# A first node as sixteen direct products, and a two-step node order at the start of a causal convolution on TensorE

**Chip, cores, metric.** One core of one Trainium2 chip. The metric is the device time of one execution in microseconds (us), median of several runs; "span" is the time from the first to the last instruction in the profiled execution, 1.7 to 3 us shorter. The mean granted TensorE clock of all runs used here lay between 0.993 and 1.000 of full speed.

## The reference

```python
# x: (8, 4096, 512) float32, kernel: (8, 512, 512) float32
out = np.zeros_like(x)
for k in range(8):
    shifted = x if k == 0 else np.concatenate(
        [np.zeros((B, k, D)), x[:, :-k, :]], axis=1)
    out += np.matmul(shifted, kernel[k])
```

A causal convolution over the sequence with eight taps, each tap a 512 x 512 matrix.

## The kernel before

Each of 128 partitions owns a run of 256 rows, worked off in 32 steps of eight rows. Within a step the 8 x 8 tap products are split three times in the Karatsuba manner: LO (taps 4 to 7), HI (taps 0 to 3) and MID, whose weights are differences of a HI and a LO weight. A step has three nodes of nine products, 27 instead of 64. A product is four matmuls of 128x512.

```python
def product(bank, comp, w, start):
    for c in range(DC):
        nc.tensor.matmul(bank, lhsT=comp[:, c * P:(c + 1) * P], rhs=w[:, c, :], ...)

def node_a1(k):                       # first product of node k
    ...
    n.q = pair(3)
    product(n.q[:, 1], n.s[1][1], W[a, MID, HI], True)
    nc.scalar.copy(out=n.q[:, 0], in_=n.q[:, 1])
```

Then come two products (`a0`, `u`), ScalarE copies that seed two PSUM pairs and fill `dts`, a buffer that the subtractions read, two more products (`v`) with a VectorE subtraction each (`d`), and four last ones (`l`). VectorE builds the sums of x rows (D4, D42, D1, D2 ...) and most of the middle weights. Halo rows are the seven rows before a partition's run; fills are matmuls with zeros at the start. x is loaded by GpSimd into `xin`, cast to bf16, and transposed by a DMA into one tile, used for every step again:

```python
XT = spool.tile([P, K, D], bf, name="XT")            # 8 rows, two halves
def transpose_x(xin, h):
    nc.sync.dma_start_transpose(out=XT[:, 4 * h:4 * h + 4, :]..., in_=xin...)
def prep_m():                                        # sums for the MID node
    tt(D1[:, 0:2], XT[:, 7::-7], XT[:, 0:2], ADD)
    ...
order = [(0, LO), (0, HI), (0, MID)]
order += [(i, a) for i in range(1, NIT) for a in (MID, LO, HI)]
```

Of the kernel before, what the change touches and what calls it, by code (L numbers as in the profile page):

```python
# [22 lines left out]
def kernel(  # L23
# [47 lines left out]
    F2 = spool.tile([P, 2, D], bf, name="F2")  # L71
    F21 = spool.tile([P, 4, D], bf, name="F21")
    F1 = spool.tile([P, 2, D], bf, name="F1")
    F0 = spool.tile([P, D], bf, name="F0")

# [3 lines left out]

    def load_x(i, h):  # L80
        xin = xpool.tile([P, 4, D], bf, name="xin")
        nc.gpsimd.dma_start(out=xin, in_=xr[:, K * i + 4 * h:K * i + 4 * h + 4, :])  # L82
        return xin

    def transpose_x(xin, h):
        nc.sync.dma_start_transpose(
            out=XT[:, 4 * h:4 * h + 4, :].rearrange("p j (c m) -> p (j c) m", m=P),
            in_=xin.rearrange("p j d -> p (j d)"))
# [47 lines left out]
    nc.gpsimd.dma_start(out=H[1:P, 4:8], in_=xr[0:P - 1, RUN - 4:RUN, :])  # L136
    x0 = [load_x(0, 0)]
    nc.gpsimd.dma_start(out=H[1:P, 1:4], in_=xr[0:P - 1, RUN - 7:RUN - 4, :])  # L138
# [12 lines left out]
    def load_w(tap):  # L151
        n = K - 1 - tap
        nc.gpsimd.dma_start(out=W[n >> 2, n >> 1 & 1, n & 1], in_=kr[:, :, tap, :])

    def mid_a(b_, c_):
        return W[MID, b_, c_], W[HI, b_, c_], W[LO, b_, c_]

    def mid_b(a, c_):
        return W[a, MID, c_], W[a, HI, c_], W[a, LO, c_]

    def mid_c(a, b_):
        return W[a, b_, MID], W[a, b_, LO], W[a, b_, HI]

    def by_dve(o, u, v):
        tt(o, u, v, SUB)

    def by_pe(o, u, v, prs):
        for h in range(2):
            pw = pair(prs[h])
            for k in range(2):  # L170
                nc.tensor.matmul(pw[:, k], lhsT=ident, rhs=u[:, 2 * h + k], start=True, stop=False)
                nc.tensor.matmul(pw[:, k], lhsT=identn, rhs=v[:, 2 * h + k], start=False, stop=True)
            nc.scalar.copy(out=o[:, 2 * h:2 * h + 2], in_=pw)

    for tap in (6, 4, 7, 5):
        load_w(tap)
    x0.append(load_x(0, 1))
    for tap in (2, 0, 3, 1):
        load_w(tap)
# [6 lines left out]
    def transpose_pe(src, k):  # L186
        o = pair(k).bitcast(bf).rearrange("p a (b d) -> p (a b) d", b=2)
        for t in range(4):
            for c in range(DC):
                nc.tensor.transpose(o[:, t, c * P:(c + 1) * P], src[:, t, c * P:(c + 1) * P], ident)  # L190
        return o

    def x_at(t):
        return (x0[0][:, t], ident) if t >= 0 else (H[:, 8 + t], identh)

    def sums_pe(k, *sums):

        pw = pair(k)
        for h, ts_ in enumerate(sums):
            for c in range(DC):  # L200
                for n, t in enumerate(ts_):
                    src, idt = x_at(t)
                    nc.tensor.matmul(pw[:, h, c * P:(c + 1) * P], lhsT=src[:, c * P:(c + 1) * P],  # L203
                                     rhs=idt, start=n == 0, stop=n == len(ts_) - 1,
                                     skip_group_check=True)
        return pw
# [4 lines left out]
    o = transpose_pe(x0[0], 0)  # L211
    nc.scalar.copy(out=XT[:, 0:4], in_=o)
    pw = sums_pe(1, (-4, 0), (-3, 1))
    nc.vector.tensor_copy(out=D4[:, 0:2], in_=pw)  # L214
    pw = sums_pe(2, (-2, 2), (-1, 3))
    nc.vector.tensor_copy(out=D4[:, 2:4], in_=pw)
    pw = sums_pe(3, (-5, -1))
    nc.vector.tensor_copy(out=D4[:, 7], in_=pw[:, 0])
    pw = sums_pe(0, (-7, -3), (-6, -2))
    nc.scalar.copy(out=D4[:, 5:7], in_=pw)  # L220
    prep_d41(LO)
    pw = sums_pe(1, (-1, 0), (0, 1))
    nc.scalar.copy(out=F1, in_=pw)
    fill(pair(3))
    tt(D42[:, 7], D4[:, 5], D4[:, 7], ADD)
    prep_d42(LO)
    pw = sums_pe(2, (-2, 0), (0, 2))
    nc.scalar.copy(out=F2, in_=pw)
    pw = sums_pe(0, (-3, -2, -1, 0), (-2, -1, 0, 1))
    nc.scalar.copy(out=F21[:, 0:2], in_=pw)  # L230
    by_dve(*mid_b(LO, HI))
    pw = sums_pe(1, (-1, 0, 1, 2), (0, 1, 2, 3))
    nc.scalar.copy(out=F21[:, 2:4], in_=pw)
    nc.scalar.copy(out=F0, in_=XT[:, 0])
    fill(pair(0))
    fill(pair(1))
    prep_d421(LO)
    by_dve(*mid_c(LO, LO))
    by_dve(*mid_b(LO, LO))
    by_dve(*mid_c(LO, MID))  # L240
    by_dve(*mid_c(LO, HI))
    xi = [load_x(1, 0)]

    mpool = ctx.enter_context(tc.tile_pool(name="m", bufs=2))
    cpool = ctx.enter_context(tc.tile_pool(name="c", bufs=2))
    ypool = ctx.enter_context(tc.tile_pool(name="y", bufs=4))
# [7 lines left out]

    class Node:
        pass

    def streams(i, a):

        if a == MID and i == 0:  # L260
            return (F0, [F1[:, 0], F1[:, 1]], [F2[:, 0], F2[:, 1]],
# [4 lines left out]
        o = 4 * a  # L266
        return (D4[:, o], [D41[:, 2 * a], D41[:, 2 * a + 1]], [D42[:, o], D42[:, o + 2]],
# [8 lines left out]
    def node_a1(k):  # L276
        n = Node()
        n.k, (n.i, n.a) = k, order[k]
# [6 lines left out]
        return n  # L285

    def node_a0u(n):
        product(n.q[:, 0], n.s[1][0], W[n.a, MID, LO], False)
        product(n.q[:, 1], n.s[0], W[n.a, MID, MID], False)

    def node_seed(n):
        for b_ in range(2):
            n.p[b_] = pair((2 * n.k + b_) % 3)
            if b_ == LO:
                nc.scalar.copy(out=n.p[b_][:, 1], in_=n.q[:, 1])  # L295
            else:
                nc.scalar.mul(out=n.p[b_][:, 1], in_=n.q[:, 1], mul=-1.0)  # L297
# [3 lines left out]
    def node_v(n, b_):  # L301
        p = n.p[b_]
        product(p[:, 1], n.s[2][b_], W[n.a, b_, MID], False)
# [17 lines left out]
    def node_e(n, b_):  # L321
        p = n.p[b_]
        if n.i == 0 and n.a == MID:
            for a in (LO, HI):
                y = first[a, b_]
                tt(y, y, p, ADD if a == LO else SUB)
                store(0, a, b_, y)
# [3 lines left out]
        else:  # L331
# [6 lines left out]
            elif n.i == 0:  # L338
                nc.scalar.copy(out=y, in_=p)
                first[n.a, b_] = y  # L340
# [5 lines left out]
    order = [(0, LO), (0, HI), (0, MID)]  # L346
    order += [(i, a) for i in range(1, NIT) for a in (MID, LO, HI)]
    nodes = [node_a1(0)]
    node_a0u(nodes[0])
    node_seed(nodes[0])  # L350
    o = transpose_pe(x0[1], 2)
    node_v(nodes[0], 0)
    node_v(nodes[0], 1)
    nc.scalar.copy(out=XT[:, 4:8], in_=o)
    xi.append(load_x(1, 1))
    prep_d4(HI)
    prep_d41(HI)
    by_dve(*mid_b(HI, HI))
    prep_d42(HI)
    for k, (i, a) in enumerate(order):  # L360
        cur = nodes[k]
        stage = k % 3
        more = i + 1 < NIT
        if stage == 0 and more:
            transpose_x(xi[0], 0)
        node_l(cur, 0, LO)
        node_l(cur, 0, HI)
        if k < 2:
            node_l(cur, 1, LO)
            node_l(cur, 1, HI)  # L370
            node_e(cur, 0)
            if k == 0:
                by_pe(*mid_a(LO, HI), (2, 0))
                node_e(cur, 1)
                fill(pair(2))
                nodes.append(node_a1(1))
                by_pe(*mid_a(HI, HI), (1, 0))
                prep_d421(HI)
                by_dve(*mid_b(HI, LO))
                by_dve(*mid_c(HI, MID))  # L380
                by_dve(*mid_c(HI, LO))
                by_dve(*mid_c(HI, HI))
                by_dve(*mid_b(MID, HI))
                by_dve(*mid_a(LO, LO))
                prep_d27()
            else:
                by_dve(*mid_a(HI, LO))
                by_dve(*mid_b(MID, LO))
                by_dve(*mid_c(MID, MID))
                by_dve(*mid_c(MID, LO))  # L390
                by_dve(*mid_c(MID, HI))
                nodes.append(node_a1(2))
                node_e(cur, 1)
        nxt = nodes[k + 1] if k + 1 < len(order) else None
        if nxt:
            node_a0u(nxt)
        if k >= 2:
            node_l(cur, 1, LO)
            node_e(cur, 0)
        if nxt:  # L400
            node_seed(nxt)
        if stage == 0:
            if i:
                prep_d421(LO)
                prep_d41(HI)
        elif stage == 1:
            if more:
                prep_m()
            if i:
                prep_d421(HI)  # L410
# [4 lines left out]
        if nxt:  # L415
            node_v(nxt, 0)
            node_v(nxt, 1)
        if stage == 0:
            if i:
                prep_d42(HI)  # L420
                prep_d27()
        elif more:
            prep_d4(LO if stage == 1 else HI)
        if k >= 2:
            node_l(cur, 1, HI)
        if k and k + 2 < len(order):
            nodes.append(node_a1(k + 2))
        if k >= 2:
            node_e(cur, 1)
        if stage == 1 and more:  # L430
            transpose_x(xi[1], 1)
# [32 lines left out]
```

## Time and profile before

| | before |
|---|---|
| time, median | 787.41 us (6 runs, 786.54 to 788.66) |
| span | 784.1 us |
| TensorE busy, matmuls | 770.0 us, 3680 |
| first product starts | 21.48 us |
| nothing but TensorE in the chain from | 65.91 us |
| VectorE waits for transposed x, whole run | 8.0 us |

The lines that the prediction shows are in its text below. First the SyncE queue, which issues the transposes and the stores (start, length, engine, line, operation):

```profile
37.53 19.09 SPq L86 DMA_TRANSPOSE XT<-xin  x2
56.67 9.01 SPq L317 DMA_DIRECT2D out_dram<-y  x4
65.80 4.40 SPq L86 DMA_TRANSPOSE XT<-xin  x1
...
79.30 3.24 SPq L86 DMA_TRANSPOSE XT<-xin  x1
...
87.34 4.88 SPq L86 DMA_TRANSPOSE XT<-xin  x1
```

Then one line of the list of waits (engine, line, what it waited for: us in total, times, longest):

```profile
DVE D L77 <- DMA XT<-xin: 8.0, 11, 1.9
```

Before, VectorE waits for transposes a little, eleven times in 784 us, and not once between 60 and 112 us, where the three transposes of the last lines land.

### The profile page before, as it was taken

Reading aid. Unit: us, or ns where it says so; the run is one execution under the profiler, and the core shown is the slowest. Engines: PE = TensorE matmul, PEld = TensorE weight load, DVE = VectorE, ACT = ScalarE, POOL = GpSimd, SP = SyncE. Lnnn points to the kernel's source line nnn. Section 1 sums busy time; section 2 is a strip of 40 time slices with the busy share of each in tenths; the row PEclk is TensorE's granted clock in tenths of the full one; section 3 lists DMA queues with packets and bytes.
Section 4 is the critical chain, followed back from the end, with each engine's and each line's share of the span. In section 5 each row is a group of like instructions: output and inputs, shape, how many; then the busy total and the mean of one; then the engine's idle time right before and its main releaser. Section 6 shows DMA issues by size and latency. Waiting matters only on the chain.

```text
span 784.1 us, 9632 instructions
## 1 busy us (share of the span) xinstructions
PE 770.0 (98%) x3680; PEld 352.7 (45%) x3680; DVE 658.2 (84%) x756; ACT 284.4 (36%) x463; POOL 42.7 (5%) x83
## 2 busy tenths in 40 slices
PE   8889999999999999999999999999999999999997
PEld 5334444444444444444444444444444444444443
DVE  4799888888888988888888888888888888888895
ACT  3543333233333333333333333333333333333332
POOL 5000000000000000000000000000000000000000
PEclk9999999999999999999999999999999999999999
DMA  9948887787888777877887877777778878787843
GB/s 165 206 88 204 180 197 183 167 180 168 177 199 194 169 184 167 176 188 185 175 201 162 187 178 198 158 193 172 176 188 187 183 171 179 166 192 185 199 129 128
DMA packets 161309, 138.89 MB, mean 177 GB/s; under 512 B 132210, under 2 KB 136306, under 8 KB 161264
## 3 DMA queue, kind: packets, MB, share of 16 engines
q1 hardware_dynamic: 147392, 99.37, 45.9%
q0 software_dynamic: 13728, 38.66, 31.8%
q8 instruction: 28, 0.46, 0.2%
q10 hardware_dynamic: 144, 0.26, 0.1%
q14 instruction: 17, 0.14, 0.1%
HBM read 77.32 MB, written 67.11 MB: 184 GB/s over the span
## 4 chain that ended last, share of the span: by engine, by line
PE 92%; DMA 4%; DVE 2%; issue 1%; POOL 0%; ACT 0%; DVEq 0%; ACTq 0%; POOLq 0%
PE pp L251 92%; DMA w<-in_kernel_dram 4%; DVE w L77 1%; DVE y L77 1%; DVE D L77 0%; DVE pp L77 0%; ACT pp L295 0%; POOL D L136 0%; DVE pp L307 0%; DVEq L459 0%; ACT pp L283 0%; POOL D L138 0%; POOL identn L146 0%; POOL ident masks.py:199 0%; POOL identh L143 0%
## 5 line engine op out<-in xcount | busy, mean ns | idle before, releaser
L251 PE MATMUL pp<-w,D 128*128 128x512 bf16 x3296 | 719.0, 379 | 3.2 <-DVE pp L77 1.2
L251 PEld LDWEIGHTS <-D 128*128 128x128 bf16 x3296 | 322.1, 98 | 393.6 <-issue 4.1
L77 DVE TENSOR_TENSOR D<-D 128x1024 bf16<-128x1024 bf16 (+1 forms) x256 | 232.0, 947 | 0.1
L77 DVE TENSOR_TENSOR y<-pp,ms 128x1024 f32<-128x1024 f32 (+1 forms) x125 | 151.5, 1213 | 47.6 <-PE pp L251 47.5
L77 DVE TENSOR_TENSOR D<-XT 128x2048 bf16<-128x2048 bf16 (+2 forms) x157 | 146.6, 950 | 9.5 <-DMA XT<-xin 8.0
L283 ACT COPY pp<-pp 128x512 f32<-128x512 f32 x96 | 54.8, 570 | 260.1 <-PE pp L251 260.1
L295 ACT COPY pp<-pp 128x512 f32<-128x512 f32 x96 | 54.7, 570 | 175.2 <-PE pp L251 171.2
L77 DVE TENSOR_TENSOR pp<-dts,pp 128x512 f32<-128x512 f32 x96 | 66.4, 692 | 49.0 <-ACT dts L299 45.3
L330 ACT COPY ms<-pp 128x1024 f32<-128x1024 f32 x62 | 63.0, 1016 | 34.2 <-PE pp L251 34.2
L82 POOL DMA_DIRECT2D xin<-in_x_dram x64 | 33.9, 530 | 690.6 <-DMA XT<-xin 679.3
L307 DVE SCALAR_TENSOR_TENSOR pp<-pp,dts 128x512 f32<-128x512 f32 x96 | 66.7, 695 | 3.7
L299 ACT COPY dts<-pp 128x512 f32<-128x512 f32 x96 | 58.0, 604 | 0.0
L297 ACT ACTIVATE pp<-pp 128x512 f32<-128x512 f32 x96 | 56.5, 589 | 0.1
L251 PE MATMUL pp<-w,XT 128*128 128x512 bf16 x124 | 31.8, 379 | 0.0
L77 DVE TENSOR_TENSOR w<-w,w 128x2048 bf16<-128x2048 bf16 x17 | 20.2, 1220 | 2.1 <-DMA w<-in_kernel_dram 2.0
L251 PEld LDWEIGHTS <-XT 128*128 128x128 bf16 x124 | 12.1, 98 | 14.6
L184 PE MATMUL pp<-zero,ident 128*128 128x512 bf16 x24 | 8.8, 519 | 4.5 <-POOL ident masks.py:199 3.6
L251 PE MATMUL pp<-w,F 128*128 128x512 bf16 x36 | 8.7, 379 | 1.4 <-ACT pp L283 0.7
L214 DVE CAST D<-pp 128x1024 bf16<-128x1024 f32 x1 | 1.2, 1225 | 8.6 <-PE pp L203 8.6
L203 PE MATMUL pp<-ident,xin 128*128 128x128 bf16 x80 | 7.5, 219 | 0.0
L184 PEld LDWEIGHTS <-ident 128*128 128x128 bf16 x24 | 2.9, 127 | 9.1 <-issue 5.2
L203 PE MATMUL pp<-identh,D 128*128 128x128 bf16 x72 | 6.9, 219 | 0.0
(37 smaller groups left out, 63.2 us busy)
## 6 DMA issues: line engine op xcount, KB each, us to landing
out_dram<-y SPq DMA_DIRECT2D x127, 512.0 KB, 3.4
xin<-in_x_dram POOLq DMA_DIRECT2D x64, 512.0 KB, 6.0
w<-in_kernel_dram POOLq DMA_DIRECT2D x8, 512.0 KB, 17.1
XT<-xin SPq DMA_TRANSPOSE x62, 6.1
D<-in_x_dram POOLq DMA_DIRECT2D x1, 508.0 KB, 5.5
D<-in_x_dram POOLq DMA_DIRECT2D x1, 381.0 KB, 8.8
out_dram<-y ACTq DMA_DIRECT2D x1, 256.0 KB, 2.1
out_dram<-y SPq DMA_DIRECT2D x1, 256.0 KB, 2.2
```

Source lines behind the costliest of these rows:

```text
L77: nc.vector.tensor_tensor(out=o, in0=a, in1=b, op=op)
L82: nc.gpsimd.dma_start(out=xin, in_=xr[:, K * i + 4 * h:K * i + 4 * h + 4, :])
L184: nc.tensor.matmul(pw[:, h], lhsT=ident, rhs=zero, start=True, stop=True)
L203: nc.tensor.matmul(pw[:, h, c * P:(c + 1) * P], lhsT=src[:, c * P:(c + 1) * P], rhs=idt, start=n == 0, stop=n == len(ts_) - 1, skip_group_ ...
L214: nc.vector.tensor_copy(out=D4[:, 0:2], in_=pw)
L251: nc.tensor.matmul(bank, lhsT=comp[:, c * P:(c + 1) * P], rhs=w[:, c, :], start=start and c == 0, stop=c == DC - 1, skip_group_check=True)
L283: nc.scalar.copy(out=n.q[:, 0], in_=n.q[:, 1])
L295: nc.scalar.copy(out=n.p[b_][:, 1], in_=n.q[:, 1])
L297: nc.scalar.mul(out=n.p[b_][:, 1], in_=n.q[:, 1], mul=-1.0)
L299: nc.scalar.copy(out=n.dts, in_=n.q[:, 0])
L307: nc.vector.scalar_tensor_tensor(out=p[:, 0], in0=p[:, 1], scalar=-1.0, in1=n.dts, op0=MUL, op1=SUB)
L330: nc.scalar.copy(out=ms[b_], in_=p)
```

## The change

Its intent: TensorE should start with the first tap that lands instead of waiting for weight differences. The first node becomes a direct four-tap product. So that the later taps 0 to 3 have time to land, the LO and HI nodes of steps 0 and 1 are done before both MID nodes, and the set-up work of VectorE and ScalarE is placed between products by hand.

```diff
+    def direct(m, t):
+        n = K // 2 - 1 - m
+        product(n0.p[t // 2][:, t % 2], D4[:, t - m] if t >= m else E4[:, 4 + t - m],
+                W[LO, n >> 1, n & 1], m == 0)
-    order = [(0, LO), (0, HI), (0, MID)]
-    order += [(i, a) for i in range(1, NIT) for a in (MID, LO, HI)]
+    order = [(0, LO), (1, LO), (0, HI), (1, HI), (0, MID), (1, MID)]
+    order += [(i, a) for i in range(2, NIT) for a in (MID, LO, HI)]
 ... (cut: the loads, now taps 4, 5, 6, 7, x, x, taps 2, 0, 1, 3; sums for two steps)
+    node_u(nodes[5])                 # reads XT row 0, the last reader of step 1's first half
 ... (cut)
+    transpose_x(2, 0)                # step 2, first half, into the same rows
 ... (cut: six output adds and their six stores lie between)
+    transpose_x(2, 1)
 ... (cut)
+    pool, name = ((ypool, "y"), (mpool, "ms"), (ypool, "y"), (fpool, "f"))[n.k]
```

The last line says where the partial outputs of the four early nodes wait for their MID node. The steady loop from step 2 on is the one of before.

## The prediction

> **What bounds the kernel now.** I read the page's busy table and slices first, then the chain that ended last, then the timeline of TensorE and of VectorE over the first 90 us. The page says that TensorE is the bound and that only its beginning is loose:
>
> ```profile
> PE 770.0 (98%) x3680; PEld 352.7 (45%) x3680; DVE 658.2 (84%) x756; ACT 284.4 (36%) x463; POOL 42.7 (5%) x83
> ...
> PE   8889999999999999999999999999999999999997
> ...
> PEclk9999999999999999999999999999999999999999
> ```
>
> Only the first three of 40 slices fall under 9 tenths, and the clock is full. The chain in order of time shows what the beginning hangs on (start, length, what):
>
> ```profile
> 4.58 9.43 DMA w<-in_kernel_dram
> 14.02 0.28 issue
> 14.30 20.72 DMA w<-in_kernel_dram
> ...
> 36.37 4.73 DVE w L77 x5
> ...
> 65.91 24.13 PE pp L251 x111
> ```
>
> The last tap lands at 35.0 us, VectorE makes weight differences from it, and only from 65.91 on does nothing but TensorE stand in the chain. TensorE's timeline has the idle time in brackets:
>
> ```profile
> 21.48 1.02 PE L251 MATMUL pp<-w,D 128*128 128x512 bf16 x4
> 23.39 1.04 PE L251 MATMUL pp<-w,D 128*128 128x512 bf16 x4 [0.88 <-DVE w L77]
> ...
> 43.13 3.61 PE L251 MATMUL pp<-w,D 128*128 128x512 bf16 x16 [1.23 <-DVE pp L77]
> ...
> 48.32 1.89 PE L251 MATMUL pp<-w,F 128*128 128x512 bf16 x8 [0.71 <-ACT pp L283]
> 50.87 1.89 PE L251 MATMUL pp<-w,F 128*128 128x512 bf16 x8 [0.66 <-ACT pp L295]
> ...
> 65.91 13.98 PE L251 MATMUL pp<-w,D 128*128 128x512 bf16 x64 [0.17 <-ACT pp L295]
> ```
>
> The first product starts at 21.48, and eight or so waits lie between it and 65.91. The 64 matmuls at 65.91 give the pace: (13.98-0.38)/63 = 0.2159 us; the stretches 100 to 400 and 400 to 700 us give 300/1391 = 0.2157. I take 0.2158, so a product (four matmuls) is 0.863 us and the whole old product work, 32 steps x 3 nodes x 9 products x 4 = 3456 matmuls, is 745.8 us.
>
> **The span of before as a sum**: first product 21.48 + products 745.8 + insertions after that point (16 transposes 0.89, 16 identity matmuls for two weight differences 3.45, two fill matmuls 0.43) 4.77 + last matmul's drain 0.16 + tail after TensorE 4.55 (779.55 to 784.1) = 776.8. The span is 784.1, so stalls cost about 7.3 us, nearly all before 65.91.
>
> **When the taps land.** VectorE's timeline shows the landings where it waits for them:
>
> ```profile
> 19.55 1.23 DVE L77 TENSOR_TENSOR w<-w,w 128x2048 bf16<-128x2048 bf16 x1 [0.18 <-DMA w<-in_kernel_dram]
> 22.10 3.62 DVE L77 TENSOR_TENSOR w<-w,w 128x2048 bf16<-128x2048 bf16 x3 [1.32 <-DMA w<-in_kernel_dram]
> ...
> 35.11 7.03 DVE L77 TENSOR_TENSOR w<-w,w 128x2048 bf16<-128x2048 bf16 x6 [0.50 <-DMA w<-in_kernel_dram]
> ```
>
> The first weight is in at 14.0 (chain), the third at 19.5, the fourth at 22.1, and five bulk loads later (x and four taps) the last at 35.0: one load each 2.6 us. The DMA row stands at 1.0 to 1.25 of its engines until 40 us, so this is a rate and not a latency.
>
> **What the Trainium skill says.** (1) "TensorE: Matmul & The Clock Gate", Back-to-back issue gap: warm spacing is N/2.4 + 2.5 ns, 216 at N=512 and 56 at 128. The trace agrees: 0.2158, and 16 transposes in 1.06 us are (1.06-0.22)/15 = 0.056 each. (2) "VectorE: DVE Perf Modes", The perf-mode tier table: a two-operand bf16 op from SBUF runs at 2x, 1224 ns for 2048 elements, at 1x once PSUM is an operand. The trace agrees: 1218 ns for a weight difference, 1.21 us for only 1024 elements out of PSUM. (3) "DMA: Bandwidth & Descriptors", SWDGE vs HWDGE vs iDMA: a DMA that casts must come from GpSimd. In this trace all x and tap loads do, in one queue, and land in issue order, so a load moved forward delays each one behind it by 2.6 us.
>
> **The change, part by part.** The built program's instruction order says what moves.
>
> *Start.* The first node no longer needs weight differences: 16 direct products instead of 9, the first of them with tap 4, which is now loaded first. TensorE before it: 16 fills (one DMA issue less stands before the identity, so they end at about 9.3 instead of 9.9), two sums 9.6 to 11.4, x transposes to 12.3, halo transposes to 13.0, then a wait for tap 4 at 14.0. First product about 14.1: gain 7.4 us.
>
> *Cost.* 7 more products = 28 matmuls = 6.0 us. So on TensorE the direct form alone almost pays back the early start; what is left is 1.3 us.
>
> *Insertions after the first product.* 24 halo-sum matmuls 1.34, two fills 0.86, 32 transposes 1.78: 4.0 us instead of 4.8. The 16 identity matmuls for weight differences are gone (3.45 us); VectorE makes all 19 differences instead of 17, so it gains two times 1.22 us.
>
> *Floor.* 14.1 + 3484 x 0.2158 (751.9) + 4.0 + 0.16 + 4.55 = 774.7. With no stall at all the change would be worth 9.4 us of span. From there it is a question of stalls.
>
> *Loads.* Order is now taps 4, 5, 6, 7, x(0, second half), x(1, first half), taps 2, 0, 1, 3. At 14.0 for the first and 2.6 each: 16.8, 19.5, 22.1, 24.7, 27.3, 29.9, 32.4, 35.0, 37.6. The last tap comes 2.6 us later than before, but 25 products of two LO nodes (21.6 us) now lie ahead of the first HI node.
>
> *Stalls, from walking the order with these durations* (four matmuls 0.863; ACT PSUM copies 0.57 and 1.01, starting about 0.5 and 0.9 apart, 1.87 for 2048; VectorE about 1.16 per weight difference, 0.6 per 1024 bf16 elements or 512 from PSUM, 1.14 per 1024 from PSUM):
> - TensorE reaches the transposes of x(0, second half) at 22.8, which lands at 24.7: 1.9 us.
> - The second transpose group needs its bank back from the 1.87 us ScalarE copy, and the first product of node 1 needs VectorE's sums at 32.6: together 0.6.
> - Node 2 starts with differences of taps 3 and 1: VectorE finishes them at 39.0, TensorE wants them at 41.5: no wait for the late taps. Small waits at seeds, the middle weight of HI, the difference of node 2 held up by the DMA transpose of x(1, second half) (lands 40.2 plus some 5 us): 0.8.
> - VectorE is busy from 27.6 to about 88 with hardly a gap in this walk. The MID weights are ready at 58.7, 59.8, 61.0 and 62.1, which is when TensorE asks for them: 0.7.
> - Node 5's second seed needs the bank that VectorE empties by two output adds until 68.8: 1.0. The MID stage ends with four pairs of output adds where before had two, and node 6 and 7 wait for seeds and D41: 0.9.
> Sum 5.9 us. TensorE then finishes its 76th product at about 89.5 and runs free.
>
> *Sum.* 774.7 + 5.9 = 780.6 of span. The time stands over the span by 2.1 us in the profiled run (786.18 to 784.1) and by 3.2 against the median; with 2.7 that is 783.3. My walk rounds waits up and the order looks hand-fitted to measured gaps, so I go 1.3 us below it: 782.0, or 0.7% less.
>
> **Rivals.** (a) *All gaps close*: the order puts products between all set-up steps, so TensorE could run nearly dry of waits from 14.1. For it: each wait of before named above has work put before it. Against: the x wait of 1.9 us is set by the DMA rate, and the halo sums and fills are few. It gives 774.7 + 2 + 2.7 = 779.4. (b) *VectorE becomes the bound until 88 us*: for it, 84% busy as a whole, 39.55 of 44.5 us busy in 21.4 to 65.9 already, and now two more differences, x sums that ScalarE and TensorE made before, and the PSUM casts. If each of the some 60 ops costs 0.05 us more than I put, 3 us are added: 786.3. Against: TensorE holds a product or two of slack at most seeds. (c) *Late inputs*: x(1, second half) and both halves of step 2 now share queue and transposes with output stores; a transpose that lands some 3 us late holds VectorE in order, and all behind it: 785 to 786. For it: GpSimd's longest waits are for transposes. Against: these freed buffers only for prefetch, and TensorE did not wait. (d) *The taps' rate differs with the new order*: each 0.1 us per load moves x(0, second half) by 0.4.
>
> **Range and chances.** Floor with the x wait 779 and the bad end of (b) or (c) 786 give 778.5 to 786. Faster by over 2% would need under 771.6, below even the stall-free 777.4 (774.7 + 2.7); slower by over 2% needs 803, 20 us of new stalls. So within 2% has 0.97.
>
> **What would show it.** First product at 14.0 to 14.3; 3620 matmuls; a TensorE idle of 1.5 to 2.2 us before the transposes near 24.7, put down to the x load; VectorE without gaps of note from 28 to 85 us; TensorE's small waits on ScalarE seeds and VectorE sums adding to 5 to 7 us; the steady pace unchanged and the tail 4.5 us. The prediction is wrong if the first product comes much after 14.3, if one wait over 2 us for a DMA or a weight difference appears after 40 us, or if the steady part (after 90 us) has changed its pace.

## The result

The changed kernel takes 787.18 us (6 runs, 786.19 to 788.11) against 787.41 us. The ratio is 0.9995 with a 95% interval of 0.9982 to 1.0008: the same. (Ratios here are the mean time of one kernel's runs over the mean of the other's in the same rounds, so not quite the ratio of the medians.) The predicted range of 778.5 to 786.0 was missed above.

The page of the changed kernel, busy table and TensorE's 40 slices:

```profile
PE 767.3 (98%) x3620; PEld 349.0 (44%) x3620; DVE 659.3 (84%) x762; ACT 281.2 (36%) x458; POOL 42.8 (5%) x83
...
PE   7899999999999999999999999999999999999997
```

There are 60 matmuls less, 3 us less of modelled busy time, and the same span (784.4). TensorE's timeline, idle time before an entry in brackets (here and in the next view the last entry ends with the window asked for):

```profile
14.27 1.89 PE L214 MATMUL pp<-w,D 128*128 128x512 bf16 x8 [1.51 <-DMA w<-in_kernel_dram]
...
25.17 1.07 PE L191 MATMUL pp<-ident,xin 128*128 128x128 bf16 x16 [2.06 <-DMA xin<-in_x_dram]
...
78.58 1.02 PE L214 MATMUL pp<-w,D 128*128 128x512 bf16 x4 [0.63 <-ACT pp L270]
80.85 8.87 PE L214 MATMUL pp<-w,D 128*128 128x512 bf16 x40 [1.25 <-ACT pp L272]
90.17 8.82 PE L214 MATMUL pp<-w,D 128*128 128x512 bf16 x40 [0.46 <-DVE D L76]
100.75 0.59 PE L214 MATMUL pp<-w,D 128*128 128x512 bf16 x2 [1.76 <-DVE pp L76]
```

The start is what it was meant to be: first product at 14.27, one wait for x. But waits remain until 100.75, where before ran freely from 65.91. The chain that ended last, in order of time, says why:

```profile
59.52 7.15 PE pp L214 x33
66.68 6.00 DMA XT<-xin
...
80.65 6.34 DMA XT<-xin
...
88.39 8.72 DMA XT<-xin
...
100.75 29.31 PE pp L214 x135
```

Three DMA transposes stand in it one after another: step 2's first half, its second half, step 3's first half. They take 21 of the 34 us from 66.68 to 100.75; the rest is work that they released (VectorE's sums and output adds, the copies and products behind them). VectorE's timeline shows it waiting at each:

```profile
72.70 2.96 DVE L76 TENSOR_TENSOR D<-XT 128x1024 bf16<-128x1024 bf16 x3 [1.90 <-DMA XT<-xin]
...
87.09 1.23 DVE L76 TENSOR_TENSOR D<-XT 128x2048 bf16<-128x2048 bf16 x1 [0.50 <-DMA XT<-xin]
...
97.13 1.83 DVE L76 TENSOR_TENSOR D<-XT 128x1024 bf16<-128x1024 bf16 x2 [2.93 <-DMA XT<-xin]
```

The same line of the list of waits as above, now of the changed kernel:

```profile
DVE D L76 <- DMA XT<-xin: 14.8, 14, 2.9
```

**Where the lead went.** From node 6 (step 2, MID) on, both kernels do the same nodes in the same order, so the start of the same node compares them directly. I read it from ScalarE's timeline: the start of the copy that follows a node's first product. A node without waits takes 7.77 us (nodes 12 to 13 of either kernel).

| node | before | changed | lead |
|---|---|---|---|
| 6 | 77.39 | 74.57 | 2.8 |
| 7 | 85.16 | 81.97 | 3.2 |
| 8 | 92.93 | 91.60 | 1.3 |
| 9 | 100.71 | 99.08 | 1.6 |
| 10 | 108.48 | 108.77 | -0.3 |
| 95, the last | 769.27 | 769.55 | -0.3 |

The change is 2.8 us ahead when it enters the steady loop and gives all of it back within four nodes. After that nothing changes any more; the 0.3 us is the difference of the spans.

**The transposes come no earlier.** The same three transposes, in both traces:

| transpose | before: starts, lands, VectorE reads | changed: starts, lands, VectorE reads |
|---|---|---|
| step 2, first half | 65.80, 72.3, 72.42 | 66.68, 72.67, 72.70 |
| step 2, second half | 79.30, 84.4, 84.45 | 80.65, 86.99, 87.09 |
| step 3, first half | 87.34, 93.8, 95.74 | 88.39, 97.11, 97.13 |

(The landings of before are the start plus the time to landing that the DMA view gives: 6.5, 5.1 and 6.5 us.) Before, VectorE came for two of the three just as they landed. The changed kernel enters 2.8 us ahead, but its transposes start 0.9 to 1.4 us later than before. So a lead in the products turns into waiting.

### The profile page after: what moved, and what is told of

It reads as the page before. It is cut to its first block, busy times and chain, and to the rows that moved or that the text cites. A ratio compares the mean times of both kernels' runs of the same rounds, so it can differ in the third digit from the quotient of the medians.

```text
span 784.4 us, 9508 instructions
## 1 busy us (share of the span) xinstructions
PE 767.3 (98%) x3620; PEld 349.0 (44%) x3620; DVE 659.3 (84%) x762; ACT 281.2 (36%) x458; POOL 42.8 (5%) x83
## 4 chain that ended last, share of the span: by engine, by line
PE 92%; DMA 5%; DVE 1%; POOL 1%; issue 0%; ACT 0%; DVEq 0%; SPq 0%; POOLq 0%
PE pp L214 91%; DMA XT<-xin 3%; DMA xin<-in_x_dram 2%; DVE D L76 1%; POOL w L80 0%; DVE y L76 0%; PE pp L191 0%; ACT XT L390 0%; POOL D L80 0%; DVE pp L76 0%; DVEq L629 0%; ACT pp L270 0%; POOL xin L80 0%; DVE f L76 0%; POOL identn L148 0%
## 5 line engine op out<-in xcount | busy, mean ns | idle before, releaser
L76 DVE TENSOR_TENSOR D<-D 128x1024 bf16<-128x1024 bf16 (+2 forms) x251 | 228.3, 949 | 0.1
L76 DVE TENSOR_TENSOR y<-pp,ms 128x1024 f32<-128x1024 f32 (+1 forms) x121 | 146.4, 1212 | 44.6 <-PE pp L214 44.5
L76 DVE TENSOR_TENSOR D<-XT 128x2048 bf16<-128x2048 bf16 (+2 forms) x155 | 143.4, 942 | 16.1 <-DMA XT<-xin 14.8
L76 DVE TENSOR_TENSOR w<-w,w 128x2048 bf16<-128x2048 bf16 x19 | 22.6, 1217 | 3.2 <-DMA w<-in_kernel_dram 3.0
L185 PE MATMUL pp<-zero,ident 128*128 128x512 bf16 x20 | 6.6, 484 | 3.1 <-POOL ident masks.py:199 3.1
L214 PE MATMUL pp<-w,w 128*128 128x512 bf16 x36 | 8.6, 379 | 0.0
L80 POOL DMA_DIRECT2D w<-in_kernel_dram x8 | 6.0, 768 | 1.9 <-DMA w<-in_kernel_dram 1.8
L191 PE MATMUL pp<-ident,xin 128*128 128x128 bf16 x48 | 3.2, 219 | 2.3 <-DMA xin<-in_x_dram 2.1
L214 PEld LDWEIGHTS <-w 128*128 128x128 bf16 x36 | 3.4, 98 | 3.8
```

Source lines behind the costliest of these rows:

```text
L76: nc.vector.tensor_tensor(out=o, in0=a, in1=b, op=op)
L80: nc.gpsimd.dma_start(out=out, in_=src)
L185: nc.tensor.matmul(pw[:, h], lhsT=ident, rhs=zero, start=True, stop=True)
L191: nc.tensor.transpose(o[:, t - t0, c * P:(c + 1) * P], src[:, t, c * P:(c + 1) * P], ident)
```

## The experiments

**A caution on the clock.** The mean granted clock hides short stretches. In some of the traces TensorE, after it has waited, runs at half clock for some 3.4 us. One microsecond of the second control below (the swap in the changed kernel), a row of the view of stretches (window; busy us and instructions of TensorE, its weight loads, VectorE, ScalarE, GpSimd; then the granted clock, the DMA share and GB/s):

```profile
82.00:83.00 1.00, 1.00 (x4) 0.41 (x3) 1.00 (x3) 0.00 (x0) 0.00 (x0) 0.50 1.07 393
```

Such a stretch costs half its length, some 1.7 us (an estimate from 3.4 us at 0.50). In stretches of 4 us the traces of the two kernels and of experiments 1 to 4 show none while TensorE works, so their node times compare directly. The controls have one each (26 to 29 us, and 82 to 85 us), experiment 5 has three stretches' worth (32 to 39 and 94 to 97 us), experiment 8 two (37 to 41 and 44 to 48 us).

The theory, called T: XT is one buffer. In the new order two steps are in work at once, so the transposes of step 2 can't start before node 5, the last of the two steps, has read XT, and then the output stores and each other's readers hold them one behind the other. Rivals: V, VectorE is simply overfull there (eight output adds close together); S, the loss lies in the start.

### 1. The same transposes, but nobody waits for them

```diff
+        dst = F21 if (i, h) in ((2, 0), (2, 1), (3, 0)) else XT[:, 4 * h:4 * h + 4]
-                    [F21[:, j] for j in range(4)])      # node 4's last streams
+                    [D421[:, j] for j in range(4)])
```

> The changed kernel, but the DMA transposes of step 2 (both halves) and of the first half of step 3 write the F21 tile, which nothing reads any more (node 4 reads D421 instead); wrong result on purpose. The same DMAs run, nobody waits for them. Theory T (the missing 3.5 us are the three transposes that stand one after another in the chain from 66.7 to 97.1 us, because one XT buffer is reused): span 3 to 5 us shorter than the changed kernel's 784.4, so about 780 and a time near 783, no VectorE wait for XT between 66 and 100. Rival V (VectorE is simply overfull there: eight output adds and all the sums): span within 1 us of 784.4. Rival S (the start is what is slower than I walked): also within 1 us.

Measured: 784.57 us, ratio to before 0.9960 (0.9947 to 0.9973), span 781.8. Its output is wrong, which doesn't matter for the time. Node 9 starts at 96.51 instead of 99.08. V and S predicted no gain and fall as the main cause. The gain, 2.6 us of span, is a little under the 3 to 5 that T expected: behind the three transposes a fourth (step 3, second half) now makes VectorE wait 3.6 us, and TensorE 1.6 us at 110. The run also lets the first transpose start at 50.2 instead of 66.7 us, since no reader holds F21: it removes the late start together with the wait.

### 2. A ring of three half steps for XT (correct)

```diff
-    XT = spool.tile([P, K, D], bf, name="XT")
+    XT = spool.tile([P, 12, D], bf, name="XT")
+    def xo(i, h):                     # first row of half h of step i
+        return 4 * ((2 * i + h) % 3)
-            out=XT[:, 4 * h:4 * h + 4, :]...
+            out=XT[:, xo(i, h):xo(i, h) + 4, :]...
-    cpool = ctx.enter_context(tc.tile_pool(name="c", bufs=2))
+    cpool = ctx.enter_context(tc.tile_pool(name="c", bufs=1))
```

The third half step takes 4 KiB per partition (four rows of 512 bf16). One `dts` buffer and the copy X0, which the ring makes needless, give back 2 KiB each, so the tiles need no more room than before.

> The changed kernel with XT as a ring of three half steps instead of two (correct result; dts has one buffer and the copy X0 is gone to make room). The first transpose of step 2 no longer needs node 5's product out of XT row 0 and may start about 63.7 instead of 66.7; the second still stands behind the stores in the SP queue. T: one or two of the three transposes leave the chain, span 2 to 4 us shorter than 784.4 (780.4 to 782.4). V or S: within 1 us.

Measured: correct, 784.81 us, ratio 0.9969 (0.9947 to 0.9991), span 781.4. Its runs spread from 783.61 to 789.21, with mean clocks of 0.994 to 1.000; the longest has the lowest. Node 8 starts at 89.39 (changed kernel: 91.60), node 10 at 105.64 (108.77). That is T's expected 2 to 4 us. The first transpose of step 2 now starts at 64.0, VectorE no longer waits for step 2, and one of the three transposes is left in the chain:

```profile
83.89 10.08 DMA XT<-xin
```

**The control for the smaller `dts` pool**, the changed kernel with that line alone:

> Control for the ring of three: the changed kernel with one dts buffer instead of two and nothing else. All theories: the same as the changed kernel within 0.5 us (span 784 to 785).

Measured: 786.31 us, ratio 0.9986 (0.9973 to 0.9999), span 784.4, node 10 at 108.19. Up to about 1 us of time, or 0.6 at node 10, may belong to that line or to chance; the ring's 3.1 us at node 10 does not. The control shows one thing more: a half-clock stretch at 26 us put its node 6 at 75.64, 1.1 us later than in the changed kernel, and node 10 came no later. What is lost before node 6 does not reach node 10; that too speaks against S.

### 3. The ring, and the second transpose ahead of the stores

```diff
     transpose_x(2, 0)
+    transpose_x(2, 1)
...
-    transpose_x(2, 1)                 # formerly behind the stores in the queue
```

> As the three-slot ring, and the second transpose of step 2 is issued directly behind the first, ahead of the output stores in the SP queue. T: VectorE meets both halves in place, span 3 to 5 us shorter than the changed kernel (779.4 to 781.4), time about 782.5; if the queue order alone mattered, this is at least 1.5 us better than the ring without it. V or S: within 1 us of 784.4.

Measured: correct, 784.43 us, ratio 0.9958 (0.9942 to 0.9974), span 782.2. The gain of 2.2 us misses T's 3 to 5, and the run is not better than the ring without the move, so in the ring the queue order was not what still held it. (Queue order alone, with the single XT, was not run. The changed kernel's trace suggests that little was to be had: VectorE waited only 0.50 us for that half, at 87.09.) Two lines show what came up in its place, of ScalarE's and of TensorE's timeline:

```profile
85.76 1.01 ACT L319 COPY ms<-pp 128x1024 f32<-128x1024 f32 x1 [4.98 <-DMA out_dram<-ms]
...
87.32 7.93 PE L219 MATMUL pp<-w,D 128*128 128x512 bf16 x36 [2.01 <-ACT pp L275]
```

Node 6 puts its output into the `ms` buffer in which node 1's output still waits to be written out; the store was issued at 77 us and has landed at 85.7. ScalarE is held 5 us, and the seed behind it holds TensorE 2.0 us.

### 4. The ring, the early transpose, and other buffers for the early outputs

```diff
-            pool, name = ((ypool, "y"), (mpool, "ms"), (ypool, "y"), (fpool, "f"))[n.k]
+            pool, name = ((mpool, "ms"), (ypool, "y"), (ypool, "y"), (fpool, "f"))[n.k]
```

The `ms` buffers, needed first, now hold the outputs that are stored first.

> The ring of three with the early transpose, and node 0's outputs in the ms buffers, node 1's in y buffers (swapped): the stage that reuses ms at 83 us then finds buffers stored at about 70 instead of waiting 5.0 us for a store issued at 77. T with this wait as the next one in the row: the 2.0 us TensorE wait at 87.3 goes, span 780 to 781 (782.2 without the swap). If the wait only hid another behind it: 781.5 to 782.5.

Measured: correct, 782.84 us, ratio 0.9943 (0.9930 to 0.9956), span 780.0. The TensorE wait is gone, from 78.15 on it runs through:

```profile
78.15 20.97 PE L219 MATMUL pp<-w,D 128*128 128x512 bf16 x96 [0.30 <-ACT pp L275]
```

Node 10 starts at 104.39, 4.1 us ahead of before. The ring with the swap but with the transpose behind the stores was not run, so what part the early transpose has in this is not known. This version beats both kernels, by 4.8 us (0.6%) against the median of before in the same rounds.

**The same swap in the changed kernel with its single XT:**

> The changed kernel with only the swap of the ms and y buffers, XT as it is. Theory T (transposes are the chain, the ms wait came up only once they were gone): no gain, span within 0.5 us of 784.4. If the buffer that waits for its store were a cause of its own from the start: 1.5 to 2.2 us shorter.

Measured: 786.22 us, ratio 0.9983 (0.9968 to 0.9998), span 784.3, node 10 at 108.58 (108.77). The profile alone would not settle it, since its half-clock stretch at 82 us costs some 1.7 us. The runs do: at a clock of 0.997 the span is 785.2 against 785.0 to 785.9 for the changed kernel, at 0.999 it is 784.3 against 784.0. So the swap alone does not give the 1.5 to 2.2 us. The two waits stand in a row: the transposes hide the buffer's.

### 5. Seven direct products left out

```diff
-    direct(2, 3)
-    direct(2, 0)
-    direct(1, 0)
-    direct(3, 0)
-    direct(3, 3)
-    direct(2, 2)
-    direct(3, 2)
```

> The changed kernel with seven of the sixteen direct products left out (those behind the second x load; wrong result on purpose), so the first node costs nine products as before. If TensorE's work bounds the stretch from 25 to 40 us, the span is 6.0 us shorter (28 matmuls of 0.2158). If VectorE's chain from the x load to the sum D41 (ready at 32.6 us) bounds node 1, TensorE waits there some 4.5 us instead, and the span is only 1 to 2.5 us shorter. Under T what is gained at 40 us moves the product that frees XT by the same amount.

Measured: 788.26 us, ratio 1.0007 (0.9990 to 1.0024). Its output is wrong, which doesn't matter for the time. Nothing gained, where the matmuls left out are worth 6.0 us. TensorE waits instead: 3.13 us for x, 1.09 for ScalarE's copy of it, 2.07 and 0.71 for VectorE before node 1, and 0.66 twice around ScalarE copies that products had covered, 8.3 us where the changed kernel has 2.3. That is the 6.0 us that was left out: in this stretch the seven extra products fill time in which TensorE would have waited. But x also landed 1.2 us later, and the waits were followed by half clock, from 32 to 39 and again from 94 to 97 us, which costs some 5 us (an estimate: 10.2 us at 0.50). So the run shows what filled the gap, not what nine products at full clock would take.

### 6. The direct node alone, in the old order

Two builds. The first changes only the first node and the order of the LO taps:

```diff
-    for tap in (6, 4, 7, 5):
+    for tap in (4, 5, 6, 7):
+    def direct(m):
+        n = 3 - m
+        for t in (2, 3, 1, 0):
+            product(p0[t // 2][:, t % 2], D4[:, (t - m) % 8], W[LO, n >> 1, n & 1], m == 0)
-    nodes = [node_a1(0)]
+    direct(0) ... direct(3)           # between the x sums and transposes
```

> The kernel before with only the first part of the change: node 0 as sixteen direct products, tap by tap, with taps loaded 4, 5, 6, 7; order of nodes, XT and all else as before. T: the first product starts near 15 instead of 21.5, but seven more products (6.0 us) follow and the HI node still waits for taps 0 to 3 (last landing 35 us) and VectorE's differences from them, so the start of node 2 (47.7 in the kernel before) moves by less than 1 us either way, span 783 to 785.5. If the direct node by itself were the gain: 1.3 to 3 us shorter, 781 to 783.

Measured: correct, 791.25 us, ratio 1.0049 (1.0036 to 1.0062). A miss, and partly of my own making: VectorE stood still for 7.1 us until 34.62, because the HI sums overwrite D4 rows that the direct products still read. The second build puts those rows elsewhere and leaves out sums that the direct form doesn't need:

```diff
-    nc.scalar.copy(out=D4[:, 5:7], in_=pw)
-    prep_d41(LO)
+    nc.scalar.copy(out=E4[:, 1:3], in_=pw)        # E4 = W[MID, MID, HI]
-    prep_d421(LO)
```

> The direct node in the old order again, built better: in the first such run VectorE stood still for 7.1 us because the sums of the HI node overwrite the D4 rows that the direct products still read as the rows before the run. Here those rows lie in a tile of their own (the middle weight tile, as in the changed kernel), the LO sums of step 0 that only the old first node needed are left out, and the second half of x(0) is transposed two taps earlier. T: what is left is 6.0 us of extra products against the same landing of taps 0 to 3: start of node 2 within 1.5 us of 47.7 as in the kernel before, span 783 to 786. If the direct form with the old node order had been enough: 781 to 783.

Measured: correct, 788.25 us, ratio 1.0013 (0.9997 to 1.0030), span 786.9; node 2 starts at 50.21 instead of 47.70. Both miss what T expected (within 1.5 us of 47.70, span 783 to 786), to the slow side. So in this build the direct form by itself is worth nothing, or costs a little: it begins earlier, is 6 us longer, and the HI node behind it waits for the same taps. What lead the change had at node 6 needs the new order. Both builds are mine, and a better placing of the set-up work may exist.

### 7. The x load ahead of tap 7

On top of experiment 4:

```diff
-    load_w(7)
-    load_x(0, 1)
+    load_x(0, 1)
+    load_w(7)
+    mid_dve(2, LO, HI)                # moved up, into VectorE's idle time
     mid_dve(1, LO, HI)
...                                    # direct(2, 3) ahead of direct(3, 1), and so on
```

> The previous one, and the second half of x(0) loaded ahead of tap 7, one LO difference made in VectorE's 3 us of waiting at 17 to 20, products placed to match. If the 2.0 us wait for that load is worth its length: 1 to 1.5 us less than the previous one, span 779 to 780. If VectorE bounds 28 to 60 us and the load order only moves the wait to tap 7: within 0.5 us of the previous one.

Measured: correct, 782.88 us, ratio 0.9945 (0.9932 to 0.9958), span 780.2: the same as without. The wait for x, 1.69 us in experiment 4, has only moved. TensorE's timeline and one line of VectorE's:

```profile
23.07 1.06 PE L196 MATMUL pp<-ident,xin 128*128 128x128 bf16 x16
...
32.06 2.76 PE L219 MATMUL pp<-w,D 128*128 128x512 bf16 x12 [1.13 <-DVE D L75]
...
40.08 19.59 PE L219 MATMUL pp<-w,D 128*128 128x512 bf16 x88 [0.85 <-DVE pp L75]
```

```profile
24.83 1.23 DVE L75 TENSOR_TENSOR w<-w,w 128x2048 bf16<-128x2048 bf16 x1 [2.98 <-DMA w<-in_kernel_dram]
```

TensorE no longer waits for x at 25, but VectorE waits 3.0 us for tap 7, and TensorE waits 1.13 and 0.85 us for VectorE afterwards. Node 4 starts at 54.59, no earlier than without the move (54.12). From 28 to 66 us VectorE is busy 37.6 of 38 us in experiment 4, which fits the expectation that VectorE bounds this stretch. But the same view has TensorE busy 37.8 of 38, so which of the two holds it is not shown.

### 8. Two weight differences on GpSimd

If VectorE is that full, work should leave it. On top of experiment 4:

```diff
-    mid_dve(0, HI, HI)
-    mid_dve(0, LO, HI)
     load_x(2, 1)
+    for w in ((0, HI, HI), (0, LO, HI)):
+        o, u, v = mid(*w)
+        nc.gpsimd.tensor_tensor(out=o, in0=u, in1=v, op=SUB)
```

> The ring of three with early transpose and swapped buffers (span 780.0), with two of the nineteen weight differences (taps 4 from 0 and 6 from 2) made by GpSimd between its loads instead of by VectorE at 47 to 52. If VectorE's total from 28 to 78 us sets what is left (small waits of TensorE between 40 and 60, 0.8 us in all, and 1.3 us at the seeds of nodes 5 and 6): 1 to 2 us shorter, span 778 to 779. If TensorE itself bounds that stretch and the seeds wait for other things: within 0.5 us. If the two engines hold each other up: longer.

Measured: correct, 790.76 us, ratio 1.0040 (1.0025 to 1.0055), span 787.6: 8 us worse than experiment 4. GpSimd's line, then two of VectorE's:

```profile
32.59 8.35 POOL L445 TENSOR_TENSOR w<-w,w 128x2048 bf16<-128x2048 bf16 x2 [2.65 <-DMA w<-in_kernel_dram]
```

```profile
32.75 4.28 DVE L75 TENSOR_TENSOR D<-D,w 128x512 bf16<-128x512 bf16 x1
36.95 5.07 DVE L75 TENSOR_TENSOR w<-w,w 128x2048 bf16<-128x2048 bf16 x1
```

A VectorE sum that takes 0.42 us elsewhere took 4.28, a weight difference of 1.22 took 5.07, each about as long as one of GpSimd's two differences (4.2 us) or until it was done. The Trainium skill says so in "SBUF — State Buffer", Who interferes with whom: a VectorE instruction with two SBUF inputs contends with a GpSimd instruction that reads SBUF, and the second to start is blocked. This trace agrees. TensorE waited 2.29 and 2.08 us for the held sums and then ran twice at half clock, some 3.4 us lost (an estimate: 6.9 us at 0.50); node 2 starts at 46.65 instead of 39.12. The run says nothing about what VectorE's load is worth, because it was raised and not lowered; that stays open.

## Why the prediction was wrong

- **The bound, the landings, the floor**: right. First product 14.27 us (14.1 predicted), 3620 matmuls, the x wait 2.06 us at 25.17 (1.9 at 24.7), the last seed of node 5 at 68.31 (its bank free at 68.8), the pace as before.
- **The direct node's cost of 6.0 us**: right as a count. Experiment 6 agrees that alone it pays back nothing; experiment 5 suggests that in the new order the extra products stand where TensorE would have waited.
- **The start's stalls**: right in sum. The first product of node 6 is the 60th; the prediction's terms put its end at 14.1 + 60 x 0.863 + 4.0 + 5.0 (the stall items before it) = 74.9, and its copy started at 74.57. In part this is luck: the small waits put at 0.8 and 0.7 hardly show (TensorE is busy 39.20 of the 39.21 us from 28.19 to 67.40).
- **The step that failed** is the last stall item, "The MID stage ends with four pairs of output adds where before had two, and node 6 and 7 wait for seeds and D41: 0.9", with the sentence after the sum: "TensorE then finishes its 76th product at about 89.5 and runs free". The 76th product is the first of node 8. Its copy started at 91.60, and it did not run free: node 10 began at 108.77, where 89.5 plus two nodes of 7.77 is 105.0. The term was 3.7 us too small, and the span is 3.8 us over the predicted sum (784.4 to 780.6). What stood there was chiefly the three transposes in a row: in experiments 1, 2 and 4 the same output adds remain, and TensorE's waits of 1.25 and 1.76 us at 80.85 and 100.75 shrink to one of 0.85 (ring) or are gone.
- **The error behind it** is in rival (c). It named the thing, a transpose that holds VectorE by some 3 us (measured 2.93), though its time, 785 to 786, was still 1.2 us too low at the upper end. I set it aside because "these freed buffers only for prefetch, and TensorE did not wait". That was read from the old order, where the MID node, the one that reads XT itself, comes first in each step. In the new order step 1's MID node comes last and holds row 0 of XT until 66.7 us, so the next transposes start no earlier than before while the products are 2.8 us ahead: a prefetch becomes a wait. The old trace had the warning, rows landed at 72.3 and read at 72.42. I followed the stalls until node 6 and took the rest to be as before. The prediction's own signs of being wrong came true: VectorE has gaps of 1.90 and 0.82 us between 28 and 85 us, and a wait of over 2 us for a DMA (2.93) after 40 us.
- **The step down by 1.3 us** because the order "looks hand-fitted" had no number behind it, and made it worse. Without it the range still would have had to reach higher.
- **Rival (b), VectorE as the bound**: not what cost the time; experiment 1 shortened the run without taking anything off VectorE. Whether it holds the start from 28 to 66 us is not shown: it is full there, but so is TensorE (experiment 7), and experiment 8 raised its load instead of lowering it.
- With the transposes and the `ms` wait out of the way (experiment 4) the profiled span is 780.0 (the six runs: 779.9 to 782.9), within 0.6 us of the sum in the prediction. The sum was about that of a kernel with half a step more room for XT and a free output buffer.
- **Small misreadings** that cost nothing: the last of the 40 slices stands at 7 too (the tail). The 1.21 us op quoted for PSUM has float32 operands, so it doesn't separate PSUM from float32. And the section that it quotes for the spacing of matmuls gives that formula for an isolated one, and about 131 ns for a sustained stream at N=512; the 0.2158 us measured sides with the formula.

## What to carry to other kernels

When a change keeps more of something in flight, list every buffer that is refilled by a transfer, and find its last reader in the new order: the transfer starts there, however early its rows are wanted. Compare the same later work item in both traces to see where a lead is lost, and don't stop walking at the point where the new code joins the old loop. After one wait is gone, expect the next one behind it: here a single XT, then an output buffer awaiting its store. And look at the granted clock in short stretches: here a wait of 1 to 3 us could be followed by 3.4 us at half clock, and so cost twice.

## What the Trainium skill lacked or had wrong

- "DMA: Bandwidth & Descriptors", Latency and other measured facts: it gives 261 GB/s for a DMA transpose, from which 512 KiB would take 2.0 us (an estimate, without a fixed cost). The fastest seen here landed after 4.3 us. Next to stores and loads, the three transposes in the chain took 6.0, 6.3 and 8.7 us, and the median to landing over the run was 6.2. The page has no figure for a transpose that shares the engines. Nor has its Bandwidth section one for casting loads queued one behind another: here 2.6 us each for 1 MiB read and 512 KiB written.
- "GPSIMD Engine Reference", Engine selection: it calls GpSimd about 2x slower on two-input operations (its own measured pair is float32). Here the operands are bf16: two weight differences took 8.35 us there, 4.2 each, against 1.22 on VectorE (3.4 times), and stopped VectorE meanwhile.
